# A hybrid HGRN2 / RWKV-7 / cross-attention layer on one core: six weight tiles taken in two passes over the tokens, one inverse product by halves, HGRN products regrouped, and a new order of all instructions

## The chip, the core and the metric

The kernel runs on one core of a Trainium2 chip. The metric is the device time of one execution in microseconds, the median over several runs. The engines are named as the profile names them: PE (TensorE, matrix products), PEld (its weight loads), DVE (VectorE), ACT (ScalarE), POOL (GpSimd) and SP (SyncE, which issues the DMAs).

## The reference, cut to what matters

One layer of a streaming encoder runs over a prompt of 1024 tokens and a sample of 32 tokens (1056 columns in all), width 1024, in fp32.

```python
def layer(x, mk, mv, hg_s0, rw_s0, shift0, lb, lw):
    n = rmsnorm(x, lw['norm_mix'])
    p = n @ lw['w_in']                                   # 1024 x 3840: HGRN columns, then RWKV columns
    hg_o, hg_s = hgrn2_mixer(p[..., :HG_COLS], ...)      # chunked recurrence, 4 heads of 128
    rw_o, rw_s, rw_shift = rwkv7_mixer(p[..., HG_COLS:], ...)   # 8 heads of 64; token shift, delta rule
    x = x + jnp.concatenate([hg_o, rw_o], axis=-1) @ lw['w_out']
    x = x + cross_attend(rmsnorm(x, lw['norm_cross']), mk, mv, lw['w_cq'], lw['w_co'])
    n = rmsnorm(x, lw['norm_ffn'])
    x = x + (jax.nn.silu(n @ lw['w_ff1']) * (n @ lw['w_ff3'])) @ lw['w_ff2']
    return x, hg_s, rw_s, rw_shift
```

`mk, mv` of the prompt are `rmsnorm(mem) @ w_k` and `@ w_v`. Both mixers carry a state from token to token; the RWKV one needs, per chunk of 64 tokens, the inverse of a triangular 64x64 matrix.

## The kernel before, in words

**Recording and planning.** The program is written as ordinary code on a `Graph`, which only records nodes. A PE node is a run of matmuls up to the next instruction of another engine or an explicit `cut`. `plan` then makes one list for every engine by simulating the five engines with fixed prices (`price`, `DELAY`): at each step it takes the ready node with the longest remaining path (`n.path`), with a bias per group of work (`BIAS`). `latest` turns a finished plan into latest start times, which serve as ranks of the next plan (`PASSES` times), and `nudged` adds a pseudo-random shift to the ranks of all nodes that are due after a given moment, one shift for each entry of `NUDGE` (moment, seed, reach). So these numbers set the order on every engine. On the chip every engine works its list strictly in that order. Because everything is emitted in one helper, all instructions carry one line number in the profile; groups are told apart by tiles and shapes. `f`, `mb`, `r`, `rw`, `wr` are regions of SBUF, `bank` is a bank of PSUM.

**Large products.** A weight tile of 128 columns (`load_w`) is fetched into `wr` (512 KB), rounded by ACT to fp32r (`hi`, in `rw`), and POOL computes the rest (`lo`, in `rw`). `gemm` adds three fp32r products for each k: hi·hi, hi·lo, lo·hi, so a tile of `w_in` takes 24 matmuls for each of the three token blocks of 352 (`BLOCKS`). There are two buffers each for `wr`, `hi` and `lo` (`FIFO`). `w_in` has 30 such tiles, 14 of which are RWKV ones; `rw_proj` mixes each block with the previous token (`mix`), which needs the last column of the block before (`edge`).

**Start.** `load_rows` fetches nine row tiles of x (128 tokens each, the last 32), takes the sum of squares on ACT, the power -1/2 on POOL (`rstd_pow`), scales by it and by the gain row `norm_mix` (a broadcast DMA of its own) on DVE, transposes on PE, and splits into hi (ACT) and lo (DVE).

**Mixers.** `lora` projects two RWKV tiles. `rwkv(j)` (j = 0, 2; two heads pairs each) first projects six tiles (r, k, v), then goes through five segments (four of 256 tokens, one of the sample's 32), each with a triangular `inverse` (five levels of small products, fp16 but for the last, which are fp32) and a serial chain over four chunks. `hgrn(i)` (i = 0..3) projects four tiles and goes through five segments as well; in a segment of 256 tokens it makes, for each of two groups of 128, one product of full size, two with 32 columns and one with 64.

**After the mixers.** `memory_kv` (fp32r, 256 columns; weights in `rw`), `out_proj` and `cross` (352 columns), the feed-forward part (264 columns), and the final norm. `memory_kv` may start once the regions that hold the normalized x are free, that is after the last projection of `w_in`; `out_proj` needs all mixers.

Of the kernel before, what the change touches and what calls it, by code (L numbers as in the profile page):

```python
# [21 lines left out]
KD = D // 128  # L22
# [12 lines left out]
LATER = 10.0  # L35
PASSES = 1
START, NUDGE = (291, 0.5), ((0, 3825, 0.6), (480, 1426, 0.2), (660, 4358, 1.5), (720, 1344, 0.6), (840, 6345, 3), (1200, 2280, 1.5), (1560, 9149, 3), (1620, 5315, 0.2), (1680, 6266, 12), (1740, 8928, 1.5),)
KEEP = 1.5 * BIAS
# [153 lines left out]
class Node:  # L192
    def __init__(self, graph, eng):
        self.eng, self.i = eng, len(graph.nodes)
        self.calls, self.cost, self.late = [], 0.0, 0.0
        self.preds, self.bufs, self.unit, self.bias, self.phase = {}, {}, graph.unit, graph.bias, graph.phase
        self.port = self.dense = False
        graph.nodes.append(self)
# [10 lines left out]
def shake(i, seed):  # L209

    return (i * 2654435761 + seed * 40503 * 65537 >> 7) % 1021 / 1020 if seed else 0.0
# [91 lines left out]
class Graph:  # L303
# [148 lines left out]
    def plan(self, rank):  # L452
# [29 lines left out]
        for n in nodes:  # L482
            n.path = n.path - n.bias + START[1] * shake(n.i, START[0]) if rank is None else -rank[n]
        engines = ("tensor", "vector", "scalar", "gpsimd", "sync")
# [223 lines left out]
class Net:  # L708
# [183 lines left out]
    def load_rows(self):  # L892
# [4 lines left out]
        gain = self.w2("grow")  # L897
        nc.sync.dma_start(gain, self.i["norm_mix"].to_broadcast([128, D]))
        for ap, n, t0 in self.rows():
# [579 lines left out]
    def mixers(self):  # L1479
        nc = self.nc  # L1480
        self.load_rows()
        self.params()
        self.last = self.mc.tile([128, 28], F32, name="last")
        self.lora()
        self.scratch_h()
        self.diag_n, self.diag = 0, []
# [44 lines left out]

    def proj(self, col, mix=None, bias=BIAS):

        nc = self.nc
        nc.bias = bias
        w = self.load_w(self.i["w_in"][0, :, col:col + 128], KD, eng=nc.gpsimd)

        def evac(t0, n, ps):
            t = self.tmp([128, TB], "pe")[:, :n]
            nc.scalar.copy(t, ps)  # L1540
            nc.sync.dma_start(self.p_dram[:, col // 128, t0:t0 + n], t)

        self.gemm(w, self.xact, KD, mix or evac)
        nc.bias = 0.0

    def rw_proj(self, tile, done=None, bias=BIAS):

        nc = self.nc
        V, S = nc.vector, nc.scalar
        mu, edge = self.P("mu", tile), None  # L1550

        def mix(t0, n, ps):
            nonlocal edge
            m = self.tmp([128, TB], "mixed")[:, :n]
            keep = self.P("omu", tile)
            c = min(TP - t0, n)
            if t0:
                S.activation(m[:, 0:1], ps[:, 0:1], AF.Identity, scale=keep, bias=edge)
                S.activation(m[:, 1:n], ps[:, 1:n], AF.Copy, scale=keep)
            else:  # L1560
                S.activation(m, ps, AF.Copy, scale=keep)
            V.scalar_tensor_tensor(m[:, 1:c], ps[:, 0:c - 1], mu, m[:, 1:c], ALU.mult, ALU.add)
            if c == n:
                edge = self.tmp([128, 1], "edge")
                S.activation(edge, ps[:, n - 1:n], AF.Copy, scale=mu)
# [9 lines left out]

        self.proj(2048 + 128 * tile, mix, bias)

# [29 lines left out]
    def rwkv(self, j):  # L1607
        nc = self.nc
        V, S, G, PE = nc.vector, nc.scalar, nc.gpsimd, nc.tensor
        half = (slice(0, 64), slice(64, 128))  # L1610
        for tile in (j, 4 + j, 8 + j):
            for a in range(2):
                self.rw_proj(tile + a)
        ht = None
# [206 lines left out]
    def inverse(self, am, nc_):  # L1821
# [26 lines left out]
        def product_diag(left, right):  # L1848
# [6 lines left out]
            return ps  # L1855

        def place(dst, ps, mask):
            V.tensor_tensor(dst.rearrange("p c (h u) -> p c h u", h=2),
                            ps.unsqueeze(2).to_broadcast([128, nc_, 2, 64]),
                            mask.unsqueeze(1).to_broadcast([128, nc_, 2, 64]), ALU.mult)  # L1860
# [12 lines left out]
        for l in range(1, 6):  # L1873
# [6 lines left out]
            if l < 5:  # L1880
                S.copy(x, ps)
        V.tensor_tensor(p, product(abd, y32), bc(self.i64), ALU.add)
        V.tensor_tensor(y1, product(xbd, p), y32, ALU.add)
# [9 lines left out]
    def hgrn(self, i):  # L1893
# [6 lines left out]
        for s in range(5):  # L1900
# [75 lines left out]
            for g in range(ng):  # L1976
# [4 lines left out]
                vk.append(self.u("hvk").rearrange("p (a u) -> p a u", a=2))  # L1981
                S.copy(vk[g][:m], ps[:m])
            for g in range(ng):
                gl = slice(128 * g, 128 * g + m)
                am = self.ah[self.ah_n % 3]
                self.ah_n += 1
                ams.append(am)
                ps = self.psm.tile([128, 128], F32, tag="m", name="ps_ha")
                PE.matmul(ps[:m, :m], lhsT=kg[:, gl], rhs=qg[:, gl], start=True, stop=True)
                if m == 128:  # L1990
                    PE.matmul(ps[0:32, 32:64], lhsT=kk[:, g, 0], rhs=qe[:, g, 1], start=True, stop=True)
                    PE.matmul(ps[64:96, 96:128], lhsT=kk[:, g, 2], rhs=qe[:, g, 3], start=True, stop=True)
                    PE.matmul(ps[0:64, 64:128], lhsT=kf[:, g].rearrange("p b u -> p (b u)"),
                              rhs=qf[:, g].rearrange("p b u -> p (b u)"), start=True, stop=True)
                V.copy_predicated(am[:m, :m], self.mask_h[:m, :m], ps[:m, :m])
            pkv = self.psm.tile([128, 2, 128], F32, tag="m", name="ps_kv")
# [63 lines left out]
```

## Time and profile before

| | |
|---|---|
| median of 3 runs | 1832.72 us (1831.22 to 1836.06) |
| the profiled execution | 1827.96 us, span 1826.2 us, mean granted clock 0.991 |
| PE busy | 1779.5 us, 97% of the span |
| PEld, DVE, ACT, POOL busy | 1681.4, 1264.6, 836.3, 605.7 us |
| PE waits, as the view of waits lists them | 18.3 us for DVE on `mb`, 12.3 of it at the very start |
| chain that ended last | 83% PE, 5% DVE, 3% ACT |

How to read it: busy time of PE includes time in which a pipelined matmul is stretched by a slower clock, so the granted clock has to be read beside it. The profiled execution is 4.8 us shorter than the median of the timed runs.

### The profile page before, as it was taken

What the parts mean: (1) busy time and instruction counts of PE and PEld (TensorE: products, weight loads), DVE (VectorE), ACT (ScalarE), POOL (GpSimd) and SP (SyncE); (2) the same over time, 40 slices, a digit from 0 to 9 for tenths busy, and PEclk for the clock granted to TensorE, in tenths of its full rate; (3) what the DMA queues carried; (4) which work ended last, traced back from release to release, by engine and by line L of the source; (5) the groups of instructions that cost most, each with busy time, mean ns of one, the idle gap of its engine ahead of it and who ended that gap; (6) DMA issues with size and microseconds to landing.
All of it is one profiled execution on the core that took longest, in us unless ns stands there. A gap on an engine that the chain in (4) does not pass through costs nothing.

```text
span 1826.2 us, 39245 instructions
## 1 busy us (share of the span) xinstructions
PE 1779.5 (97%) x15439; PEld 1681.4 (92%) x15439; DVE 1264.6 (69%) x2502; ACT 836.3 (46%) x1983; POOL 605.7 (33%) x764
## 2 busy tenths in 40 slices
PE   6999999999999989999999999999999999999997
PEld 5998888888989877999999999999999999999997
DVE  6246567867667879423554546998877877968996
ACT  5644446556454658533222346433333333653432
POOL 6234243443424434055000036632232223232321
PEclk9999999999999979999999999999999999999999
DMA  5244133332321346744111242232322234654522
GB/s 177 73 131 130 46 101 94 89 91 83 105 71 50 100 109 200 243 146 138 47 47 47 63 144 89 70 130 89 111 89 89 98 120 154 189 161 138 181 94 96
DMA packets 206313, 201.88 MB, mean 111 GB/s; under 512 B 18712, under 2 KB 191376, under 8 KB 206128
## 3 DMA queue, kind: packets, MB, share of 16 engines
q1 hardware_dynamic: 206128, 199.37, 35.0%
q8 instruction: 121, 1.98, 0.4%
q14 instruction: 64, 0.52, 0.1%
HBM read 139.66 MB, written 59.67 MB: 109 GB/s over the span
## 4 chain that ended last, share of the span: by engine, by line
PE 83%; DVE 5%; ACT 3%; DMA 2%; issue 1%; POOL 1%; SPq 0%; DVEq 0%; POOLq 0%; ACTq 0%
PE bank L383 83%; DVE f L383 2%; DVE mb L383 2%; ACT mb L383 2%; ACT f L383 1%; DVE rw L383 1%; DVE r L383 1%; DMA f<-p_scratch 1%; POOL mb L383 0%; ACT r L383 0%; POOL f L383 0%; ACT rw L383 0%; DMA f<-h_scratch 0%; DMA x_scratch<-mb 0%; DMA f<-in_cache_mem_k_dram 0%
## 5 line engine op out<-in xcount | busy, mean ns | idle before, releaser
L383 PE MATMUL bank<-r,rw 128*128 128x264 f32 (+1 forms) x5928 | 894.7, 305 | 4.3 <-POOL rw L383 2.0
L383 PEld LDWEIGHTS bank<-r,rw 128*128 128x128 f32 x5928 | 837.1, 188 | 13.3 <-POOL rw L383 3.2
L383 PE MATMUL bank<-mb,rw 128*128 128x264 f32 (+4 forms) x3672 | 509.6, 293 | 4.8 <-DVE r L383 1.9
L383 PEld LDWEIGHTS bank<-mb,rw 128*128 128x128 f32 x3672 | 484.2, 188 | 10.2 <-DVE rw L383 1.7
L383 DVE TENSOR_TENSOR f<-bank,f 128x264 f32<-128x264 f32 (+6 forms) x499 | 229.6, 472 | 192.6 <-PE bank L383 173.9
L383 POOL TENSOR_TENSOR f<-f 128x64 f32<-128x64 f32 (+8 forms) x205 | 115.4, 572 | 330.5 <-PE bank L383 187.8
L383 ACT CAST rw<-wr 128x512 fp32r<-128x512 f32 (+3 forms) x167 | 115.5, 697 | 211.0 <-PE bank L383 188.3
L383 DVE TENSOR_TENSOR f<-f 128x264 f32<-128x264 f32 (+8 forms) x309 | 188.5, 626 | 20.2 <-ACT f L383 13.1
L383 PE MATMUL bank<-f 128*128 128x128 f32 (+12 forms) x1374 | 193.6, 286 | 4.3 <-DVE f L383 2.5
L383 ACT ACTIVATE f<-f 128x256 f32<-128x256 f32 (+7 forms) x295 | 124.5, 447 | 114.0 <-DVE f L383 61.6
L383 PEld LDWEIGHTS bank<-f 128*128 128x128 f32 (+7 forms) x1262 | 141.5, 162 | 30.6 <-issue 6.6
L383 DVE TENSOR_TENSOR mb<-bank,f 128x1024 f16<-128x1024 f32 (+6 forms) x200 | 135.8, 705 | 44.5 <-PE bank L383 35.6
L383 PE MATMUL bank<-f,mb 64*64 64x64 f32 (+5 forms) x2248 | 122.9, 221 | 21.9 <-DVE mb L383 17.9
L383 ACT CAST rw<-r 128x512 fp32r<-128x512 f32 (+2 forms) x106 | 61.2, 577 | 116.7 <-PE bank L383 91.8
L383 DVE TENSOR_TENSOR rw<-wr,rw 128x512 fp32r<-128x512 f32 (+3 forms) x137 | 103.1, 757 | 16.5 <-ACT rw L383 15.6
L383 ACT COPY mb<-bank 128x512 f32<-128x512 f32 (+5 forms) x151 | 69.0, 467 | 89.8 <-PE bank L383 76.0
L383 POOL TENSOR_TENSOR rw<-wr,rw 128x1024 fp32r<-128x1024 f32 x30 | 72.5, 2418 | 96.6 <-ACT rw L383 66.1
L383 ACT COPY f<-bank 128x264 f32<-128x264 f32 (+8 forms) x221 | 76.0, 359 | 60.3 <-PE bank L383 44.9
L383 DVE TENSOR_TENSOR rw<-r,rw 128x512 fp32r<-128x512 f32 (+2 forms) x106 | 80.0, 755 | 23.0 <-ACT rw L383 22.2
L383 PEld LDWEIGHTS bank<-f,mb 64*64 64x64 f32 (+3 forms) x1352 | 62.1, 141 | 32.4 <-DVE mb L383 16.5
L383 ACT ACTIVATE mb<-bank,f 128x1 f32<-128x1 f32 (+5 forms) x133 | 55.4, 461 | 48.5 <-PE bank L383 45.5
L383 PE MATMUL bank<-mb 64*64 64x64 f32 (+5 forms) x1310 | 76.0, 237 | 1.1 <-ACT mb L383 1.0
(123 smaller groups left out, 1792.9 us busy)
## 6 DMA issues: line engine op xcount, KB each, us to landing
wr<-in_w_in_dram SPq DMA_DIRECT2D x30, 512.0 KB
wr<-in_w_ff_dram SPq DMA_DIRECT2D x28, 512.0 KB
p_scratch<-mb SPq DMA_DIRECT2D x80, 176.0 KB
f<-h_scratch SPq DMA_DIRECT2D x47, 264.0 KB
r<-in_w_ff_dram SPq DMA_DIRECT2D x24, 512.0 KB
h_scratch<-f SPq DMA_DIRECT2D x18, 528.0 KB
f<-x_scratch SPq DMA_DIRECT2D x15, 528.0 KB
f<-p_scratch SPq DMA_DIRECT2D x58, 128.0 KB
```

The lines of the kernel that those rows point to most:

```text
L383: getattr(eng, method)(*args, **kw)
```

## The change

`first` projects the six RWKV tiles of j = 0 in two passes: token block 0 of all six, then blocks 1 and 2 of all six. Each of these weight tiles is therefore fetched and split twice. `rwkv(0)` no longer projects. The last column of a block is kept per tile in `self.edges`. In `inverse`, the fp32 product with the block-diagonal matrix `abd` is made by two 64x64 products for each chunk instead of one 128x128 (68 chunks in all: eight full segments of 8, two of 2). In `hgrn`, the products of both groups go to one PSUM tile, all full-size ones first, then all with 32 columns, then all with 64. The DMA of the gain row gets a bonus in the plan (`soon`). `PASSES` goes from 1 to 4, and `NUDGE` from 10 entries to 41, with another start seed.

```diff
+SOON = 30
-PASSES = 1
-START, NUDGE = (291, 0.5), ((0, 3825, 0.6), (480, 1426, 0.2), (660, 4358, 1.5), (720, 1344, 0.6), (840, 6345, 3), (1200, 2280, 1.5), (1560, 9149, 3), (1620, 5315, 0.2), (1680, 6266, 12), (1740, 8928, 1.5),)
+PASSES = 4
...
-            n.path = n.path - n.bias + START[1] * shake(n.i, START[0]) if rank is None else -rank[n]
+            n.path = n.soon + (n.path - n.bias + START[1] * shake(n.i, START[0]) if rank is None else -rank[n])
...
-        nc.sync.dma_start(gain, self.i["norm_mix"].to_broadcast([128, D]))
+        nc.sync.dma_start(gain, self.i["norm_mix"].to_broadcast([128, D])).soon = SOON
...
         self.last = self.mc.tile([128, 28], F32, name="last")
+        self.edges = {}
         self.lora()
+        self.first(BLOCKS[:1], BLOCKS[1:])
...
-                S.activation(m[:, 0:1], ps[:, 0:1], AF.Identity, scale=keep, bias=edge)
+                S.activation(m[:, 0:1], ps[:, 0:1], AF.Identity, scale=keep, bias=self.edges[tile])
...
-        self.proj(2048 + 128 * tile, mix, bias)
+        self.proj(2048 + 128 * tile, mix, bias, blocks)
+
+    def first(self, *groups):
+
+        for blocks in groups:
+            for tile in (0, 1, 4, 5, 8, 9):
+                self.rw_proj(tile, bias=0.0, blocks=blocks)
...
-        for tile in (j, 4 + j, 8 + j):
-            for a in range(2):
-                self.rw_proj(tile + a)
+        if j:
+            for tile in (j, 4 + j, 8 + j):
+                for a in range(2):
+                    self.rw_proj(tile + a)
...
+        def halves_product(left, right):
+
+            ps = stacked()
+            for c in range(nc_):
+                for hf in half:
+                    PE.matmul(ps[hf, c], lhsT=left[hf, c, hf], rhs=right[hf, c], start=True, stop=True)
+            nc.cut()
+            return ps
...
-        V.tensor_tensor(p, product(abd, y32), bc(self.i64), ALU.add)
+        V.tensor_tensor(p, halves_product(abd, y32), bc(self.i64), ALU.add)
...
+            psh = self.psm.tile([128, 2, 128], F32, tag="m", name="ps_ha")
             for g in range(ng):
                 gl = slice(128 * g, 128 * g + m)
+                PE.matmul(psh[:m, g, :m], lhsT=kg[:, gl], rhs=qg[:, gl], start=True, stop=True)
+            if m == 128:
+                for g in range(ng):
+                    PE.matmul(psh[0:32, g, 32:64], lhsT=kk[:, g, 0], rhs=qe[:, g, 1], start=True, stop=True)
+                    PE.matmul(psh[64:96, g, 96:128], lhsT=kk[:, g, 2], rhs=qe[:, g, 3], start=True, stop=True)
+                for g in range(ng):
+                    PE.matmul(psh[0:64, g, 64:128], lhsT=kf[:, g].rearrange("p b u -> p (b u)"),
+                              rhs=qf[:, g].rearrange("p b u -> p (b u)"), start=True, stop=True)
+            for g in range(ng):
                 am = self.ah[self.ah_n % 3]
...
-                V.copy_predicated(am[:m, :m], self.mask_h[:m, :m], ps[:m, :m])
+                V.copy_predicated(am[:m, :m], self.mask_h[:m, :m], psh[:m, g, :m])
```

The new seeds change the order nearly everywhere. Three places follow.

On SP, at the very start of the program (x rows, the gain row, weight tiles). Before:

```order
L383 DMA mb_87<-in_x_prompt_dram 128x1024 x3
L383 DMA mb_87<-in_norm_mix_dram 128x1024
L383 DMA mb_87<-in_x_prompt_dram 128x1024
L383 DMA wr_75<-in_w_in_dram 128x8x128 x2
L383 DMA mb_87<-in_x_prompt_dram 128x1024 x3
```

Now:

```order
L384 DMA mb_87<-in_norm_mix_dram 128x1024
L384 DMA mb_87<-in_x_prompt_dram 128x1024 x4
L384 DMA wr_75<-in_w_in_dram 128x8x128
L384 DMA mb_87<-in_x_prompt_dram 128x1024
L384 DMA wr_75<-in_w_in_dram 128x8x128
L384 DMA mb_87<-in_x_prompt_dram 128x1024 x3
```

The gain row moved from the fourth place to the first, and each x row is one place later behind it.

On PE, one HGRN segment of 256 tokens late in the mixers (rows with 32x32 and the 64x64 row right behind them are its 32- and 64-column products; the `bank<-mb 64x64 x4` row ahead belongs to the RWKV chain). Before:

```order
L383 MATMUL bank_58<-mb_87 64x64 x4
L383 MATMUL bank_61<-f_0_71 128x128
L383 MATMUL bank_61<-mb_87,f_0_71 32x32 x2
L383 MATMUL bank_61<-mb_87 64x64
L383 MATMUL bank_62<-f_0_71 128x128
L383 MATMUL bank_62<-mb_87,f_0_71 32x32 x2
L383 MATMUL bank_62<-mb_87 64x64
L383 MATMUL bank_64<-mb_87,f_0_71 128x512
```

Now:

```order
L384 MATMUL bank_61<-f_0_71 128x128 x2
L384 MATMUL bank_60<-f_0_71 128x128 x2
L384 MATMUL bank_60<-f_0_71 32x32 x4
L384 MATMUL bank_60<-f_0_71 64x64 x2
L384 MATMUL bank_65<-f_0_71,mb_87 64x64 x4
```

Two rounds through the three sizes became one round in one bank.

On PE, the end of the projections of `w_in` (rows with 128x352 are projections, `128x64` with `f,mb` are products of `inverse`). Before:

```order
L383 MATMUL bank_60<-r_0_79,rw_83 128x352 x2
L383 MATMUL bank_60<-r_0_91,rw_83 128x352
L383 MATMUL bank_60<-r_0_79,rw_83 128x352
L383 MATMUL bank_62<-f_0_71,mb_87 128x128
L383 MATMUL bank_58<-f_0_71,mb_87 128x128
L383 MATMUL bank_62<-f_0_71,mb_87 128x128
L383 MATMUL bank_58<-f_0_71,mb_87 128x128
```

Now:

```order
L384 MATMUL bank_64<-mb_87,f_0_71 128x512
L384 MATMUL bank_59<-r_0_79,rw_83 128x352
L384 MATMUL bank_59<-r_0_91,rw_83 128x352
L384 MATMUL bank_59<-r_0_79,rw_83 128x352 x2
L384 MATMUL bank_59<-r_0_91,rw_83 128x352
L384 MATMUL bank_59<-r_0_79,rw_83 128x352 x2
L384 MATMUL bank_59<-r_0_91,rw_83 128x352
L384 MATMUL bank_59<-r_0_79,rw_83 128x352 x2
L384 MATMUL bank_59<-r_0_91,rw_83 128x352
L384 MATMUL bank_59<-r_0_79,rw_83 128x352
L384 MATMUL bank_63<-f_0_71 128x128 x2
L384 LDWEIGHTS mb_87
```

Before, the first products of the last full RWKV segment (its rows `f,mb 128x128`) come only after the last projection; now the last projection already stands between products of that segment's `inverse` (the row after these is `bank_62<-f_0_71,mb_87 128x64`). From the last row with 128x352 to the first row of `memory_kv` (`rw,r 128x256`), the order of PE before has 601 small matmuls, and now 254.

More of the change, by code (lines that the diff above doesn't have):

```diff
@@ L35 @@
 LATER = 10.0
-PASSES = 1
-START, NUDGE = (291, 0.5), ((0, 3825, 0.6), (480, 1426, 0.2), (660, 4358, 1.5), (720, 1344, 0.6), (840, 6345, 3), (1200, 2280, 1.5), (1560, 9149, 3), (1620, 5315, 0.2), (1680, 6266, 12), (1740, 8928, 1.5),)
+SOON = 30
+PASSES = 4
+START, NUDGE = (4291, 2), ((0, 3475, 0.2), (35, 7729, 1.5), (65, 3475, 0.2), (205, 9903, 3), (210, 1329, 0.2), (235, 4113, 0.6), (265, 1329, 0.2), (530, 1329, 0.2), (560, 9269, 0.6), (660, 4719, 0.6), (665, 8473, 0.2), (670, 9328, 12), (685, 7830, 12), (700, 636, 0.2), (705, 6641, 12), (710, 2682, 12), (715, 1121, 0.6), (720, 8195, 12), (800, 1255, 12), (845, 148, 0.6), (860, 7859, 6), (870, 6519, 0.2), (890, 8853, 12), (915, 8563, 12), (950, 7902, 12), (975, 5479, 6), (1025, 3786, 6), (1045, 3924, 6), (1090, 3786, 6), (1165, 6074, 0.2), (1235, 3786, 6), (1480, 3201, 1.5), (1540, 9428, 3), (1555, 3786, 6), (1580, 3609, 1.5), (1590, 9225, 6), (1610, 5077, 3), (1665, 1872, 1.5), (1680, 878, 6), (1740, 2277, 6), (1770, 1679, 1.5),)
 KEEP = 1.5 * BIAS
@@ L195, in __init__ @@
         self.calls, self.cost, self.late = [], 0.0, 0.0
-        self.preds, self.bufs, self.unit, self.bias, self.phase = {}, {}, graph.unit, graph.bias, graph.phase
+        self.preds, self.bufs, self.unit, self.bias, self.phase, self.soon = {}, {}, graph.unit, graph.bias, graph.phase, 0.0
         self.port = self.dense = False
@@ L1530, in s, with proj @@
         return self.sp.tile([128, 128 if dt == F32 else 256], dt, tag="s", name=name)
-    def proj(self, col, mix=None, bias=BIAS):
+    def proj(self, col, mix=None, bias=BIAS, blocks=BLOCKS):
         nc = self.nc
@@ L1541, in evac, with rw_proj @@
             nc.sync.dma_start(self.p_dram[:, col // 128, t0:t0 + n], t)
-        self.gemm(w, self.xact, KD, mix or evac)
+        self.gemm(w, self.xact, KD, mix or evac, blocks)
         nc.bias = 0.0
-    def rw_proj(self, tile, done=None, bias=BIAS):
+    def rw_proj(self, tile, done=None, bias=BIAS, blocks=BLOCKS):
         nc = self.nc
         V, S = nc.vector, nc.scalar
-        mu, edge = self.P("mu", tile), None
+        mu = self.P("mu", tile)
         def mix(t0, n, ps):
-            nonlocal edge
             m = self.tmp([128, TB], "mixed")[:, :n]
@@ L1563, in mix @@
             if c == n:
-                edge = self.tmp([128, 1], "edge")
+                edge = self.edges[tile] = self.tmp([128, 1], "edge")
                 S.activation(edge, ps[:, n - 1:n], AF.Copy, scale=mu)
@@ L1987, in hgrn @@
                 ams.append(am)
[L1988 to L1994, printed above, removed]
-                V.copy_predicated(am[:m, :m], self.mask_h[:m, :m], ps[:m, :m])
+                V.copy_predicated(am[:m, :m], self.mask_h[:m, :m], psh[:m, g, :m])
             pkv = self.psm.tile([128, 2, 128], F32, tag="m", name="ps_kv")
```

## The prediction

> **What bounds the kernel.** I read the page first, then the waits of PE, then PE by windows.
>
> ```profile
> span 1826.2 us, 39245 instructions
> PE 1779.5 (97%) x15439; PEld 1681.4 (92%) x15439; DVE 1264.6 (69%) x2502; ACT 836.3 (46%) x1983; POOL 605.7 (33%) x764
> PE bank L383 <- DVE mb L383: 18.3, 10, 12.3
> PE bank L383 <- DVE f L383: 4.9, 10, 1.1
> PE bank L383 <- DVE r L383: 3.5, 5, 1.3
> PE bank L383 <- ACT mb L383: 3.3, 6, 1.0
> PE bank L383 <- ACT f L383: 2.7, 6, 0.9
> PE bank L383 <- POOL rw L383: 2.0, 2, 1.2
> ```
>
> PE is busy for 97% of the span, and the six rows of waits (us in total, times, longest) add up to 34.7 us. So a microsecond of work taken from PE is a microsecond of time, and work put on ACT, POOL or the DMAs costs something only where PE then waits. A busy PE is not always a fast one, though, so the windows come next (length; PE, PEld, DVE, ACT and POOL busy; granted clock; DMA share and GB/s):
>
> ```profile
> 600.00:623.00 23.00, 22.89 (x200) 18.56 (x198) 18.60 (x40) 18.72 (x47) 13.19 (x18) 1.00 0.29 83
> 645.00:652.00 7.00, 5.32 (x69) 4.29 (x68) 6.93 (x11) 5.86 (x21) 2.47 (x4) 0.98 0.75 206
> 652.00:679.00 27.00, 23.59 (x176) 18.72 (x173) 18.32 (x60) 12.32 (x47) 9.06 (x32) 0.50 0.38 103
> 623.07:706.37 83.30, 75.42 (x923) 60.36 (x922) 71.57 (x198) 55.08 (x179) 32.13 (x81) 0.84 0.41 116
> 1040.00:1400.00 360.00, 358.09 (x2926) 356.75 (x2925) 280.27 (x452) 147.94 (x308) 135.58 (x103) 1.00 0.31 103
> ```
>
> Almost everywhere PE is full at clock 1.00 (the first and the last row). The exception is 623.07 to 706.37, the end of the mixers: the projections have run out, `memory_kv` has not begun, and PE lives on the small products of the last segments, which wait for DVE and ACT. It loses twice there: 83.30 - 75.42 = 7.9 us of idle time, and 27 us at half clock, whose 23.59 busy us would be 11.8 at full clock. The stretch thus holds 75.42 - 11.8 = 63.6 us of work and lasts 83.3: 19.7 us are lost. This is the largest loss of the kernel behind its start.
>
> **The change part by part.**
>
> *Inverse product by halves.* These rows stand side by side (start, duration, columns of the array, shape, count; a fp32 product leaves two records, and the next row's start tells when it is over):
>
> ```profile
> 591.37 1.15 PE L383 MATMUL bank<-f,mb 64*64 64x64 f32 x32
> 592.44 0.71 PE L383 MATMUL bank<-f 128*128 128x128 f32 x4
> ...
> 595.24 1.89 PE L383 MATMUL bank<-mb 128*128 128x64 f32 x16
> 596.97 0.40 PE L383 MATMUL bank<-f 128*128 128x64 f16 x8
> ```
>
> The product with `abd` is the third row: eight matmuls, 596.97 - 595.24 = 1.73 us. Sixteen 64x64 ones, the first row, take 592.44 - 591.37 = 1.07 us. That saves 0.66 us in each of eight full segments and, with a quarter of the matmuls, about 0.16 in each of two small ones: -5.6 us, all on PE. The bounds: -8 if the halves overlap better than in that row, -3 if entering and leaving the 64x64 shape costs more between full-size products. [...]
>
> *HGRN products regrouped.*
>
> ```profile
> 597.67 0.49 PE L383 MATMUL bank<-f 128*128 128x128 f32 x2
> 598.09 0.26 PE L383 MATMUL bank<-mb,f 128*32 128x32 f32 x4
> 598.27 0.33 PE L383 MATMUL bank<-mb 128*64 128x64 f32 x2
> 598.53 0.49 PE L383 MATMUL bank<-f 128*128 128x128 f32 x2
> 598.95 0.26 PE L383 MATMUL bank<-mb,f 128*32 128x32 f32 x4
> 599.13 0.33 PE L383 MATMUL bank<-mb 128*64 128x64 f32 x2
> 599.39 1.12 PE L383 MATMUL bank<-mb,f 128*128 128x512 f32 x2
> ```
>
> One round of three sizes takes 598.53 - 597.67 = 0.86 us, two take 1.72. Within a run of one size a narrow product costs 1.07 / 16 = 0.07 us by the row of 32 above, so the second group's three narrow ones add 0.21 to the first round. The full one takes 598.09 - 597.67 = 0.42 with the change of size behind it; as an estimate I put half of that on the product, 0.21. So 1.72 becomes 0.86 + 0.42 = 1.28, -0.44 us in each of 16 segments: -7.0 us. If changes of size were free, it would be 0; if the second group were free, -13.8. I stay in the middle, since 0.86 is about twice what its products come to. The first group's result now waits 0.4 us longer for its `copy_predicated` on DVE, with the DVE work queued behind it; PE has the projections to do meanwhile.
>
> *Six tiles in two passes.* PE makes the same matmuls. New are six DMAs of 512 KB on SP, six hi casts on ACT and six lo subtractions on POOL:
>
> ```profile
> L383 POOL TENSOR_TENSOR rw<-wr,rw 128x1024 fp32r<-128x1024 f32 x30 | 72.5, 2418 | 96.6 <-ACT rw L383 66.1 <-PE bank L383 30.2
> 14.77 1.05 ACT L383 CAST rw<-wr 128x1024 fp32r<-128x1024 f32 x1
> L383 PE MATMUL bank<-r,rw 128*128 128x352 f32 x2736 | 478.1, 328 | 3.3 <-POOL rw L383 2.0 <-DVE r L383 0.9
> 36.00:100.00 64.00, 63.18 (x395) 61.61 (x396) 21.85 (x55) 36.15 (x93) 13.53 (x11) 1.00 0.27 82
> ```
>
> POOL's 6 x 2.42 = 14.5 us and ACT's 6.3 us fall into the window 36 to 100, where POOL is busy for 13.5 of 64 us, and 3 MB are little at 82 GB/s. What is tight is the turnover. A tile in the first pass feeds PE for only 24 x 478.1 / 2736 = 4.2 us, and with two buffers the next hi and lo can start only when an older tile is done: 1.05 + 2.42 = 3.5 us, plus handing over. That just fits. Bounds: 0, and 6 x 1.2 = 7.2 us if each tile waits as long as PE's longest wait for `rw` (1.2, shown above). I take +1, near to the fit.
>
> What it buys: the first segment of `rwkv(0)` needs block 0 only, so the recurrences start about 50 us of projections earlier (six tiles times two blocks of 4.2 us), and stand beside projections to their end. In the new order 254 small matmuls instead of 601 lie between the last projection and `memory_kv`. In proportion that is 63.6 x 254 / 601 = 27 us of work. The other 37 us move forward and lie among groups of 352 columns, as in the window 600 to 623, where PE is full. If the loss shrinks with the work, 19.7 x 254 / 601 = 8 us stay and 12 are gained. The bounds: 19.7 gained, if neither wait nor half clock remains, and 0, if one half-clock period of 27 us (worth 13.6) and 6 us of waits come back on the shorter stretch. I take -12. Next late there are the last inverse's own steps on DVE and ACT, which have no projection beside them for 6 us of PE work.
>
> *Gain row sooner.*
>
> ```profile
> 4.24 2.32 POOL L383 TENSOR_SCALAR_AFFINE_SELECT f<-f 64x64 f32<-64x64 f32 x5
> 4.57 1.06 ACT L383 ACTIVATE mb<-mb 128x1024 f32<-128x1024 f32 x1 [2.51 <-DMA mb<-in_x_prompt_dram]
> 7.38 0.19 POOL L383 TENSOR_SCALAR f<-f 128x1 f32<-128x1 f32 x1
> 7.81 0.55 POOL L383 TENSOR_TENSOR f<-f 128x1 f32<-128x1 f32 x1
> 10.95 1.28 DVE L383 SCALAR_TENSOR_TENSOR mb<-mb,f 128x1024 f32<-128x1024 f32 x1 [4.13 <-DMA mb<-in_norm_mix_dram]
> 12.29 5.08 PE L383 MATMUL bank<-f,mb 128*128 128x128 f32 x24 [12.29 <-DVE mb L383]
> 18.71 3.22 POOL L383 TENSOR_TENSOR rw<-wr,rw 128x1024 fp32r<-128x1024 f32 x1
> 26.12 1.86 PE L383 MATMUL bank<-r,rw 128*128 128x352 f32 x10 [1.20 <-POOL rw L383]
> ```
>
> DVE waits for the gain row until 10.95, though POOL had the row's factor at 8.36. With the gain row first that wait goes, and POOL is late next: in its new list 14 selects of 64x64 stand ahead of the first factor, not 10, so at 0.46 us each (the first row) it comes 1.9 us later, the scaling at some 10.3 and PE at some 11.6: -0.7 us. Behind that the first matmuls still wait for POOL's lo, whose place in POOL's list hardly changes. I take -1, with -3 and +2 as ends.
>
> *The new order elsewhere.* No work goes or comes. Of the 34.7 us of waits some 17 are at the start and 7.5 in the stretch above, so 10 are left to gain, and as much could be lost: 0, with 8 either way.
>
> **The sum:** -5.6 - 7.0 + 1 - 12 - 1 + 0 = -24.6 us on a span of 1826.2, so 1801.6, or 1803.4 for the profiled execution, which took 1827.96. The median of the runs was 1832.72, 4.8 us above it; it becomes 1832.7 - 24.6 = 1808.1, so 1808.
>
> **The rivals.** *The end of the mixers gains nothing* (20%): the half clock sets in again and the waits are as long, because fewer products wait for the same chain. For it: in the row 645 to 652 a PE only 5.32 / 7.00 busy was enough to bring on half clock. Against it: less than half of that work is left. Then 1808 + 12 = 1820.
>
> *The clock stays full* (15%): the short stretch never gets thin enough, and little waits. Then the remaining 8 us go too: 1800. [...]
>
> *Slower* (6%): the first pass starves PE. If hi and lo of a tile take 5.4 us rather than 3.5 (POOL's 3.22 us of 18.71 above, behind its other work), PE waits 1.2 us in every 5.4; that is as thin as the row 645 to 652, and projections would run at half clock for 27 us, which costs 13.6. With the 7.2 us of waits this is +20.8 instead of +1. It decides only where the end of the mixers gains nothing either: -5.6 - 7.0 + 20.8 - 1 = +7.2, 1840. Above 13.6 us it outweighs what the other steps take from PE.
>
> *No change* (4%): the same with two thirds of it.
>
> **How the numbers follow.** 55% for 1808 with a range of its own of 1798 to 1819, and the others as given. The measurement tells 0.3%, 5.5 us, from no change. The first three cases are faster by more: 90%; 4% within, 6% slower. The range for 8 in 10 leaves out the slower cases and the best tenth: 1789 to 1824.
>
> **What would show it.** Right: PE busy falls by some 20 us; rows of 64*64 64x64 with 32 records stand where 128*128 128x64 f32 x16 stood; in HGRN, rows 128*128 x4, 128*32 x8, 128*64 x4 follow each other in about 1.28 us; from the last 352-column projection to the first 256-column matmul less than 40 us pass; the first PE row starts before 12.3. Wrong: waits of PE for POOL `rw` or ACT `rw` between 45 and 90 above 7 us in total; a second window of clock 0.50; or waits spread over the mixers, which would mean that the new order is tight where the prices are wrong.

## The result, and the profile after

The changed kernel takes 1803.29 us (median of four runs, 1803.02 to 1803.93) beside 1834.39 us for the kernel before (four runs, 1831.22 to 1836.55). The ratio is 0.983, 95% interval 0.982 to 0.985: 31 us faster. The forecast was 1808, in a range of 1789 to 1824. The profiled execution has a span of 1801.6 us; 1826.2 was 24.6 us longer, which is the forecast sum to the tenth. That the sum came out does not make its terms right, as the experiments show.

The head of the page of after, and the view of PE's waits (total us, times, longest us):

```profile
span 1801.6 us, 39539 instructions
PE 1760.8 (98%) x15575; PEld 1669.0 (93%) x15575; DVE 1275.2 (71%) x2502; ACT 842.1 (47%) x1989; POOL 621.8 (35%) x770
PE bank L384 <- DVE mb L384: 17.4, 9, 11.6
PE bank L384 <- DVE f L384: 4.8, 8, 1.4
PE bank L384 <- POOL rw L384: 3.4, 2, 1.8
PE bank L384 <- ACT mb L384: 2.5, 4, 1.2
PE bank L384 <- ACT f L384: 1.5, 4, 0.6
PE bank L384 <- DMA mb<-in_x_sample_dram: 1.3, 1, 1.3
PE bank L384 <- DVE rw L384: 0.8, 1, 0.8
```

PE's busy time fell by 18.7 us. The waits fell by less: all rows of the view add up to 32.4 us, against 37.4 of before (31.7 in the seven rows shown here, 34.7 in the six that the prediction shows). So the larger part of the gain is work (or slow work) that is gone from PE, not waiting.

The windows of after, with the columns as before; the third row is the stretch from the last projection to the first `memory_kv` matmul, the fourth its part at half clock:

```profile
36.00:100.00 64.00, 62.03 (x415) 59.17 (x413) 27.72 (x56) 43.22 (x97) 29.75 (x26) 1.00 0.57 171
600.00:641.47 41.47, 39.83 (x528) 35.08 (x528) 37.40 (x75) 26.64 (x68) 18.80 (x27) 1.00 0.27 74
641.47:676.70 35.23, 30.84 (x414) 23.74 (x412) 30.58 (x102) 25.58 (x91) 14.39 (x39) 0.90 0.41 120
652.90:659.70 6.80, 6.20 (x52) 4.24 (x52) 5.32 (x23) 4.40 (x18) 3.81 (x15) 0.50 0.30 92
```

The stretch lasts 35.2 us instead of 83.3, and half clock in it 6.8 us instead of 27.3. By the prediction's own reckoning 30.84 - 6.20 / 2 = 27.7 us of it are work and 7.5 are lost, where 19.7 were.

Rows of after in order of time (start, duration, columns of the array, shape, records). The first two pieces are an HGRN segment and a halves product; the row behind each tells when it is over. The last two pieces are the first pass and the start:

```profile
325.00 0.60 PE L384 MATMUL bank<-mb,f 128*128 128x128 f32 x4
325.54 0.32 PE L384 MATMUL bank<-f,mb 128*32 128x32 f32 x8
325.78 0.45 PE L384 MATMUL bank<-mb 128*64 128x64 f32 x4
326.16 0.49 PE L384 MATMUL bank<-f 128*128 128x128 f32 x2
...
587.84 1.15 PE L384 MATMUL bank<-mb 64*64 64x64 f32 x32
588.92 4.09 PE L384 MATMUL bank<-r,rw 128*128 128x352 f32 x24
...
65.80 3.80 PE L384 MATMUL bank<-r,rw 128*128 128x352 f32 x22 [1.63 <-POOL rw L384]
69.43 0.60 PE L384 MATMUL bank<-f,mb 128*128 128x128 f32 x4
69.78 4.09 PE L384 MATMUL bank<-r,rw 128*128 128x352 f32 x24
...
11.64 1.97 PE L384 MATMUL bank<-f,mb 128*128 128x128 f32 x8 [11.64 <-DVE mb L384]
14.74 1.97 PE L384 MATMUL bank<-f,mb 128*128 128x128 f32 x8 [1.13 <-DVE mb L384]
18.45 3.40 PE L384 MATMUL bank<-f,mb 128*128 128x128 f32 x16 [1.74 <-DVE mb L384]
21.60 0.57 PE L384 MATMUL bank<-r,rw 128*128 128x352 f32 x2
23.98 6.29 PE L384 MATMUL bank<-r,rw 128*128 128x352 f32 x28 [1.81 <-POOL rw L384]
```

The HGRN products now take 326.16 - 325.00 = 1.16 us, the halves 588.92 - 587.84 = 1.08. In the first pass PE waits once for POOL, 1.63 us, and from there a tile follows on a tile. At the start PE begins 0.65 us sooner, waits 4.7 us for the next rows and the first weights, and is at the projections no sooner than before, where this row starts them:

```profile
20.93 3.99 PE L383 MATMUL bank<-r,rw 128*128 128x352 f32 x14
```

### A ledger of PE's list

To see where a kernel loses, every matmul record of a trace was put beside its place in PE's list, and each pair of neighbouring matmuls was priced with the median time from start to start that the same pair has in the trace of before. The sum of the prices is the work of a list; what it took longer is lost, to waits, half clock or slower neighbours. The columns follow the program, since the same moment is another place in another order: to 40 us, from there to the last projection, the stretch up to the first `memory_kv` matmul, from there to the first `out_proj` matmul, and the rest (us, one profiled execution each):

| kernel | median | work | to 40 us | mixers | stretch | memory | rest | lost in all |
|---|---|---|---|---|---|---|---|---|
| before | 1834.4 | 1728.1 | 9.9 | 27.9 | 21.8 | 1.3 | 16.5 | 77.5 |
| after | 1803.3 | 1710.4 | 10.4 | 34.1 | 10.2 | 5.3 | 12.1 | 72.1 |
| whole | 1809.5 | 1716.0 | 9.2 | 35.0 | 10.1 | 5.4 | 12.0 | 71.8 |
| rounds | 1808.0 | 1716.7 | 10.7 | 32.9 | 10.3 | 4.6 | 11.9 | 70.4 |
| both | 1814.1 | 1722.3 | 9.2 | 33.9 | 10.2 | 3.3 | 11.7 | 68.2 |
| oldseeds | 1862.6 | 1709.8 | 12.5 | 50.6 | 11.7 | 7.4 | 49.5 | 131.8 |
| nofirst | 1848.0 | 1709.3 | 9.2 | 40.4 | 26.0 | 7.7 | 31.4 | 114.7 |
| nofirst_oldseeds | 1842.3 | 1712.7 | 12.4 | 35.0 | 20.4 | 3.3 | 35.2 | 106.3 |
| b_newseeds | 1886.7 | 1722.9 | 9.1 | 54.5 | 21.9 | 8.8 | 42.8 | 137.2 |
| with_first | 1827.0 | 1712.9 | 10.5 | 40.7 | 16.0 | 5.0 | 19.0 | 91.4 |
| without_first | 1841.3 | 1711.9 | 9.3 | 41.7 | 30.4 | 3.6 | 24.2 | 109.1 |
| bwarm | 1833.6 | 1730.5 | 9.5 | 28.6 | 16.4 | 1.3 | 18.7 | 74.5 |
| after_t | 1805.1 | 1709.2 | 9.2 | 36.6 | 10.2 | 5.6 | 12.9 | 74.7 |

The work of `whole`, `rounds` and `both` stands 5.6, 6.3 and 11.9 us above that of after, close to what their times show below.

Neither the work nor the losses hold the time ahead of PE's first matmul (12.3 us in before, 11.6 in after) and from the start of its last one on (8.4 and 7.4). The columns are also less exact than their digits. A pair that before has only in its half-clock period is priced at half clock, and most of the other kernels have some 60 pairs that do not occur in before at all. Priced instead by the same pairs outside half clock, in the traces of all these kernels, before has 1719.1 us of work and loses 10.0, 32.9, 24.5, 2.6 and 16.4 us in the order of the columns, after 1707.4 and 10.4, 36.5, 10.0, 6.2 and 11.9, and `both` has 1717.1 of work. So a difference of less than some 4 us between two rows of the table should not be relied on.

### The profile page after: what moved, and what is told of

Read it like the earlier page. It is cut to its first block, busy times and chain, and to the rows that moved or that the text cites. A ratio compares the mean times of both kernels' runs of the same rounds, so it can differ in the third digit from the quotient of the medians.

```text
span 1801.6 us, 39539 instructions
## 1 busy us (share of the span) xinstructions
PE 1760.8 (98%) x15575; PEld 1669.0 (93%) x15575; DVE 1275.2 (71%) x2502; ACT 842.1 (47%) x1989; POOL 621.8 (35%) x770
## 5 line engine op out<-in xcount | busy, mean ns | idle before, releaser
L384 PE MATMUL bank<-mb,rw 128*128 128x264 f32 (+3 forms) x3648 | 503.1, 293 | 1.0 <-DVE f L384 0.7
L384 DVE TENSOR_TENSOR f<-bank,f 128x264 f32<-128x264 f32 (+8 forms) x563 | 264.2, 485 | 188.4 <-PE bank L384 167.3
L384 DVE TENSOR_TENSOR f<-f 128x264 f32<-128x264 f32 (+8 forms) x351 | 228.4, 667 | 16.5 <-ACT f L384 9.0
L384 POOL TENSOR_TENSOR f<-f 128x264 f32<-128x264 f32 (+8 forms) x211 | 118.3, 572 | 313.0 <-DMA x_scratch<-f 194.6
L384 ACT CAST rw<-wr 128x1024 fp32r<-128x1024 f32 (+3 forms) x168 | 120.0, 718 | 209.7 <-PE bank L384 167.5
L384 PEld LDWEIGHTS bank<-f 128*128 128x128 f32 (+6 forms) x1276 | 138.3, 162 | 29.7 <-issue 7.2
L384 DVE TENSOR_TENSOR mb<-bank,f 128x256 f32<-128x256 f32 (+6 forms) x180 | 119.0, 688 | 37.1 <-PE bank L384 24.3
L384 ACT COPY mb<-bank 128x512 f32<-128x512 f32 (+6 forms) x161 | 72.2, 461 | 82.8 <-PE bank L384 73.3
L384 POOL TENSOR_TENSOR r<-r 128x512 f32<-128x512 f32 (+2 forms) x46 | 64.9, 1418 | 119.5 <-DMA r<-in_w_ff_dram 62.2
L384 ACT COPY f<-bank 128x264 f32<-128x264 f32 (+9 forms) x219 | 74.9, 362 | 59.4 <-PE bank L384 52.2
L384 PEld LDWEIGHTS bank<-f,mb 64*64 64x64 f32 (+5 forms) x1258 | 59.4, 138 | 30.9 <-DVE mb L384 17.7
L384 PE MATMUL bank<-mb,f 64*64 64x64 f32 (+10 forms) x622 | 80.7, 299 | 2.1 <-DVE f L384 1.0
```

What stands on the lines that cost most here:

```text
L384: getattr(eng, method)(*args, **kw)
```

## The experiments

**The work on PE, in the order of after.** `after_again` is the changed kernel, run on the chip of the next three. `whole` and `rounds` leave every list as the planner made it and swap only what is issued for a node: the halves become the whole product again, the HGRN products go back to two rounds. `both` does both.

```diff
 # emit (all three)
-                for method, args, kw in node.calls:
+                for method, args, kw in getattr(node, "instead", None) or node.calls:
 # whole: halves_product
                     PE.matmul(ps[hf, c], lhsT=left[hf, c, hf], rhs=right[hf, c], start=True, stop=True)
+            nc.open.instead = [("matmul", (ps[:, c],), dict(lhsT=left[:, c], rhs=right[:, c], start=True, stop=True)) for c in range(nc_)]
             nc.cut()
 # rounds: hgrn, behind the eight products
+                made = nc.open.calls
+                nc.open.instead = made[:-8] + [made[k - 8] for k in (0, 2, 3, 6, 1, 4, 5, 7)]
```

> The changed kernel itself, run beside the three below so that each can be set against it on one chip: 1803 us, as before, to within 1 us. No theory expects anything else.

> The changed kernel with its order of all instructions kept, but the last fp32 product of the inverse made again by one 128x128 product for each chunk instead of two of 64x64. Theory (the gain is PE work taken away, and PE has no slack there): the product of a full segment goes from 1.08 us to about 1.73 us, 8 x 0.65 + 2 small = +5.6 us, so 1809 us (1806 to 1811); PE's busy time rises by the same 5 to 6 us and the waits stay. Rival (the gain is a better order, the halves only fill what would be waiting): within 1.5 us of the changed kernel, 1802 to 1804.5, the longer product eating into the wait behind it.

> The changed kernel with its order kept, but the HGRN products of a full segment made again in two rounds (full size, 32, 32, 64 columns of one group, then of the other) instead of all of one size together. The same products in all. Theory (each change of the array's size costs PE time): from about 1.28 us to 1.72 us for each of 16 segments, +7.0 us, 1810 us (1807 to 1814). Rival (the grouping costs nothing by itself, what changed the time is the order around it): within 1.5 us of the changed kernel.

> Both of the edits above together, again in the order of the changed kernel. Theory (both are PE work on a path without slack, so they add): +12.6 us, 1816 us (1812 to 1820), and what is then left of the gain against the kernel before, some 15 us, is the end of the mixers and the order. Rival (they hide in each other's waits): less than 8 us above the changed kernel. Rival (order only): within 2 us of the changed kernel.

Measured: `after_again` 1802.78 us (1801.97 to 1803.62; ratio to before 0.983, 0.981 to 0.985), `whole` 1809.52 (1807.59 to 1812.56; 0.987, 0.985 to 0.989), `rounds` 1807.96 (1807.91 to 1810.53; 0.986, 0.985 to 0.988), `both` 1814.05 (1811.39 to 1821.18; 0.990, 0.988 to 0.992). So the halves are worth 6.7 us, the regrouping 5.2, both 11.3, nearly their sum. The medians mix granted clocks a little; among the runs at clock 0.997 alone (two each, one of `both`) it is 5.9, 5.8 and 9.9 us. The waits do not take it up: the losses of the four stand within 4 us of each other. The rows that answer, first of `whole`:

```profile
591.79 1.98 PE L384 MATMUL bank<-mb 128*128 128x64 f32 x16
593.58 0.73 PE L384 MATMUL bank<-r,rw 128*128 128x352 f32 x3
```

and of `rounds`, the segment shown above of after:

```profile
325.79 0.38 PE L384 MATMUL bank<-mb,f 128*128 128x128 f32 x2
326.10 0.26 PE L384 MATMUL bank<-f,mb 128*32 128x32 f32 x4
326.28 0.33 PE L384 MATMUL bank<-mb 128*64 128x64 f32 x2
326.54 0.49 PE L384 MATMUL bank<-mb,f 128*128 128x128 f32 x2
326.96 0.26 PE L384 MATMUL bank<-f,mb 128*32 128x32 f32 x4
327.14 0.33 PE L384 MATMUL bank<-mb 128*64 128x64 f32 x2
327.40 0.49 PE L384 MATMUL bank<-f 128*128 128x128 f32 x2
```

The whole product takes 593.58 - 591.79 = 1.79 us where the halves take 1.08; over the eight segments 1.70 to 1.83 against 1.08 in each. The same eight HGRN products take 327.40 - 325.79 = 1.61 us in two rounds and 1.16 in one; the medians over the 16 segments are 1.65 and 1.23. Both theories stand: this is PE work with nothing to hide it.

**Code and seeds crossed.** Four kernels, to tell what `first` does from what the new shifts do.

```diff
 # oldseeds: after with the numbers of before
-PASSES = 4
-START, NUDGE = (4291, 2), (41 entries)
+PASSES = 1
+START, NUDGE = (291, 0.5), (10 entries)
 # nofirst: after without the two passes, with its own numbers
-        self.first(BLOCKS[:1], BLOCKS[1:])
-        if j:
-            for tile in (j, 4 + j, 8 + j): ...
+        for tile in (j, 4 + j, 8 + j): ...
 # nofirst_oldseeds: both of these; b_newseeds: before with PASSES, START and NUDGE of after
```

> All code of the change, but with the one pass of planning, the start seed and the ten shifts of the kernel before. Between the last projection and the first memory matmul PE's list then has 242 small matmuls (601 in the kernel before, 254 in the changed one). Theory (the end of the mixers gains by `first`, which lets that small work go earlier beside projections): the stretch stays as short as in the changed kernel, 34 to 40 us, and the time is 1803 plus what waits the unsuited shifts leave elsewhere, 0 to 8 us: 1808 us (1803 to 1813). Rival (the new shifts made the gain of the stretch): the stretch loses 20 us again and the time is 1814 to 1820.

> The changed kernel without `first` (the six tiles are projected in one pass over the tokens at the head of rwkv(0), as before), with its own passes and shifts. 482 small matmuls are left between the last projection and the first memory matmul. Theory (what a stretch loses goes with the small matmuls left in it: 21.8 us for 601, 10.2 us for 254): about 18 us lost there, +7.6 us, less about 1 us for the second fetch and split saved: 1810 us (1806 to 1815). Rival (`first` is worth nothing there): 1802 to 1804.

> The changed kernel without `first` and with the passes and shifts of the kernel before; so only the halves, the HGRN regrouping and the gain row's bonus are left. 421 small matmuls between the last projection and the first memory matmul. Theory (losses by the small matmuls left there): about 16 us lost in the stretch, +5.5 us against the changed kernel, and 0 to 8 us of waits elsewhere: 1811 us (1806 to 1818). Against the kernel before that is -12.6 us of PE work and about -6 us in the stretch. Rival (the stretch and the waits go by seeds alone): 1821, the kernel before less the PE work.

> The kernel before with the four passes, start seed and 41 shifts of the changed one, and nothing else of it. 283 small matmuls between the last projection and the first memory matmul. Theory (losses by the small matmuls left there): the stretch loses some 11 us instead of 21.8, so -10 us, and 0 to +8 us of waits elsewhere: 1826 us (1822 to 1833). Rival (shifts fit only the code they were chosen for): 1834 to 1845, waits for DVE or POOL spread over the mixers.

Measured: `oldseeds` 1862.62 us (1861.88 to 1864.03; ratio 1.017, 1.015 to 1.019), `nofirst` 1848.03 (1845.47 to 1854.47; 1.009, 1.008 to 1.011), `nofirst_oldseeds` 1842.26 (1838.24 to 1844.76; 1.005, 1.004 to 1.007), `b_newseeds` 1886.68 (1885.36 to 1888.73; 1.030, 1.028 to 1.032). All four expectations missed by 30 to 60 us, and on the same side: any code with shifts that were not chosen for it is slower than either kernel, although the three that keep the new products have 15 to 19 us less work than before by the ledger. Where it goes is seen best where nothing was changed, from `out_proj` on. The waits of PE behind 1000 us in `oldseeds`:

```profile
PE bank L384 <- DVE rw L384: 8.6, 6, 3.6
PE bank L384 <- ACT rw L384: 7.0, 4, 2.9
PE bank L384 <- DVE f L384: 4.2, 5, 1.6
PE bank L384 <- ACT f L384: 2.1, 1, 2.1
```

and behind 980 us in after:

```profile
PE bank L384 <- DVE f L384: 0.7, 2, 0.5
PE bank L384 <- DVE r L384: 0.2, 1, 0.2
```

The same feed-forward code waits 22 us in one order and 1 in the other, 16 of it for what DVE and ACT write into `rw`, its weights, and five short periods at half clock, 20.5 us in all, go with it from `out_proj` on (granted clock 0.98 from 1400 us on, 0.99 in after). So the passes, the start seed and the shifts together are worth some 60 us to the code they were chosen for (1862.6 against 1803.3), twice the gain of the whole change, and these four kernels say little on a part of the code by its time. By place they say something: with `first`, after and `oldseeds` lose 10.2 and 11.7 us in the stretch; without it, before and the three others lose 20.4 to 26.0, whatever the shifts. And the loss does not go with the number of small matmuls left there: 283 in `b_newseeds` cost 21.9 us, 601 in before 21.8.

**Half clock and short waits.** `bwarm` is the kernel before with 15 matmuls more, laid into the waits ahead of the half clock.

```diff
+FILL = {5068: 1, 5106: 1, 5126: 2, 5134: 7, 5152: 4}    # number in PE's list: how many ahead of it
...
+                    if node.eng == "tensor":
+                        for _ in range(FILL.get(done, 0)):
+                            real.tensor.matmul(args[0], lhsT=ident, rhs=ident[:, :64], start=True, stop=True)
+                        done += 1
                     getattr(eng, method)(*args, **kw)
```

> The kernel before, in its own order, with 15 more fp32 matmuls of 128x128 by 64 columns on PE (0.22 us each, 3.4 us in all), put ahead of five matmuls for which PE waited between 646 and 658 us (1, 1, 2, 7 and 4 of them ahead of waits of 0.37, 0.33, 0.48, 1.60 and 1.02 us). Their results are overwritten by the matmul behind them; no other engine waits for them. Theory (the half clock from 651.7 to 679.0 us sets in because PE is thinly busy just before): the clock stays at 1.00 or falls for one or two records of 3.4 us as in the changed kernel (6.8 us), and the stretch is 7 to 12 us shorter: 1820 to 1827 us against 1832 to 1834. Rival (the clock is halved by something that short waits have no part in): 27 us at half clock as before and the time within 2 us of the kernel before, or up to 3 us above it for the added work.

Measured: 1833.64 us (12 runs, 1826.59 to 1839.41) beside 1831.97 (17 runs, 1827.77 to 1837.28), ratio 1.001, 0.9996 to 1.002. The windows of `bwarm`:

```profile
651.70:662.00 10.30, 9.08 (x107) 8.02 (x107) 10.19 (x24) 7.85 (x26) 2.17 (x8) 1.00 0.57 139
662.00:675.70 13.70, 13.38 (x94) 9.96 (x96) 8.05 (x33) 5.14 (x25) 5.90 (x22) 0.50 0.38 105
```

In the profiled execution, one of the two fastest of the twelve, the half clock comes 10.3 us later and lasts 13.7 us instead of 27.3; the stretch is 3 us shorter. But over the runs the mean granted clock is 0.9893 against 0.9885 of the kernel before, and no time is gained. So in this execution filling the waits moved the half clock and did not do away with it. It fits neither theory cleanly: in order of time PE had just run 10.3 us with 9.08 busy and no wait above 0.37 us (the row below) when it set in at 662.0:

```profile
660.98 0.39 PE L389 MATMUL bank<-f,mb 128*128 128x64 f16 x8 [0.37 <-DVE f L389]
```

The runs of these two kernels yield a price, though. Over the 17 of before, the time falls by 1.07 us for each 0.001 of mean granted clock (correlation -0.88); over the 12 of `bwarm` by the same 1.07 (-0.91). As 0.50 is the only other value of the granted clock in the traces of before and after, 0.001 of 1832 us is 3.7 us at half clock: as an estimate, from run to run one us more at half clock goes with 0.29 us more time.

**`first`, in orders sought for each code.** To compare with and without `first` fairly, both got four passes and shifts sought anew, from none, for 40 minutes each: random shifts were kept where the planner's own end came sooner. `after_t` adds 15 shifts found in this way to the 41 of after.

```diff
 # with_first: all code of after
-START, NUDGE = (4291, 2), (41 entries)
+START, NUDGE = (4291, 2), ((10, 6282, 1.5), (120, 2630, 0.6), (160, 2122, 0.6), (330, 4265, 3), (400, 6991, 6), (1480, 2690, 6))
 # without_first: the code of nofirst
+START, NUDGE = (4291, 2), ((0, 6220, 0.6), (720, 7371, 3), (830, 5171, 6), (855, 2373, 3), (920, 24, 12), (975, 6837, 12), (995, 3289, 3), (1440, 2492, 3))
```

> All code of the change, but instead of its 41 shifts six others, found by 40 minutes of trying shifts at random and keeping those by which the plan's own last instruction came sooner, from none at all. 288 small matmuls between the last projection and the first memory matmul. It is to be set against without_first, whose shifts were sought in the same way for as long. Theory (`first` is worth the shorter stretch, some 10 us, wherever the order suits the code): 1810 to 1816 us, 10 to 16 us below without_first. Rival (what the stretch gains is lost again among the mixers): within 4 us of without_first.

> The changed code without `first`, with eight shifts sought in the same way and for as long as those of with_first. 376 small matmuls between the last projection and the first memory matmul. Theory (`first` is worth the shorter stretch): 1822 to 1830 us; 15 to 22 us are lost in the stretch, against 9 to 12 in with_first. Rival (the stretch's gain is lost again among the mixers, and its place does not matter): 1808 to 1818, like with_first.

> The changed kernel with its 41 shifts kept and 15 more among them, sought in the same way. Theory (the order still holds some 60 us of losses, and a plan that ends sooner also runs sooner): 1797 to 1801 us against 1803, a little better than both kernels. Rival (the plan's prices are no finer than this, and what it gains is not seen on the chip): 1802 to 1806.

Measured: `with_first` 1826.97 us (1824.72 to 1831.01; ratio 0.997, 0.995 to 0.998), `without_first` 1841.32 (1838.33 to 1843.27; 1.004, 1.003 to 1.005), `after_t` 1805.10 (1804.52 to 1809.07; 0.985, 0.984 to 0.986). Both of the first two came out 11 us above their ranges, so such a short search does not reach the 41 shifts; but they stand 14.4 us apart, and the ledger shows where: 30.4 against 16.0 us lost in the stretch, the mixers ahead of it within 1 us (the rest differs by 5, though `first` changes nothing there; in the profiled executions the two are 17.7 apart, since that of `without_first` is the slowest of its five, at clock 0.981 against 0.984 to 0.986). The stretch in the windows, first of `with_first`:

```profile
645.40:688.40 43.00, 34.18 (x444) 26.81 (x444) 35.98 (x102) 29.90 (x99) 14.77 (x42) 0.80 0.26 78
```

and of `without_first`, with the part at half clock:

```profile
645.10:705.80 60.70, 50.20 (x546) 39.43 (x545) 46.58 (x130) 37.01 (x120) 18.32 (x51) 0.63 0.22 63
653.70:698.10 44.40, 35.73 (x363) 28.22 (x361) 33.82 (x98) 26.52 (x87) 15.09 (x44) 0.50 0.17 48
```

The theory holds for this pair as far as the place goes: with little more work in it (30.3 us against 27.0 by the ledger), the stretch without `first` spends 44.4 us at half clock, the one with it 17.1. The time of one pair proves less, as each code had one search only. `after_t` does not beat after: a plan that ends 2 us sooner by the planner's prices is 2 us later on the chip. Nor is that the only such case: the plan of `without_first` ends at 1788.7 us and that of before at 1793.2, but on the chip `without_first` is 7 us behind before. The changed kernel remains the fastest of all.

## Why the prediction was right, and where only its sum was

*Halves, -5.6.* Right: 6.7 us, inside the bounds of 3 and 8, or 5.9 at equal clock. The product costs 1.08 us in every full segment, between full-size neighbours too, and the 128x64 product, taken as 1.73 throughout, came to 1.70 to 1.83. These rows go from start to start, so they hold the change of shape behind the product and not the one ahead of it. Counted from the start of the matmul ahead of it, a segment takes 1.20 to 1.33 us with the halves in after and 1.81 to 1.93 in `whole`, 0.53 to 0.65 less, where the rows alone say 0.62 to 0.75. The change ahead thus costs some 0.1 us, and the eight full segments gain 4.7 us on PE, where the prediction counted 8 x 0.66 = 5.3 for them.

*HGRN, -7.0.* Right in mechanism, 5.2 us measured as time, or 5.8 at equal clock. The products themselves went from 1.65 to 1.23 us in the median, 0.42 a segment where 0.44 was forecast; 16 x 0.42 = 6.7. The other 1.5 us are within what the runs of `rounds` differ by (2.6).

*Two passes, +1.* Right in kind. PE waited 1.6 us for POOL `rw` between 36 and 100 us, and the ledger finds 2.0 us more lost between 40 and 80. POOL had the cover that was named: it was busy 29.75 of the 64 us, 16.2 more than before.

*End of the mixers, -12.* The number was hit: 7.5 us stay lost by the prediction's reckoning, 8 were forecast. The reason was half right. That `first` brings it is borne out by place: 10.1 to 16.0 us are lost in every order with it, 20.4 to 30.4 in every one without, but for `bwarm`, where the added matmuls bring it down to 16.4. By time it rests on one pair (14.4 us, some 5 of which lie behind the mixers). That the loss shrinks in proportion to the small matmuls left is wrong: 283, 376, 421, 482 and 601 of them lost 21.9, 30.4, 20.4, 26.0 and 21.8 us without `first`. And the gain does not stay whole: in the ledger after loses 6.2 us more than before among the mixers and 4.0 more in `memory_kv`, where the work that was moved away now stands (3.6 and 3.6 by the prices outside half clock). Up to `out_proj` after loses 60.0 us against 60.9, or 63.1 against 70.0 by those prices, so most of what the stretch gained is gone again, or half of it. "The other 37 us move forward and lie among groups of 352 columns, as in the window 600 to 623, where PE is full" is therefore the step that failed: with the work there, 7 to 10 us more are lost. Whether moving the work costs this or the new order does is not shown; between `with_first` and `without_first`, the mixers lose 1.0 us less with `first` and `memory_kv` 1.4 more.

*Gain row, -1.* PE began at 11.64 us, forecast 11.6. But nothing is left of it at 40 us: with the time ahead of PE's first matmul, 11.6 + 10.4 = 22.0 us are lost by then, and 12.3 + 9.9 = 22.2 before. POOL was late next, as forecast. The first weights' lo came 2 us later: it let PE go on at 23.98 us, where before it was done at 18.71 + 3.22 = 21.93. Of the x rows only the first three went one place later on SP. No run leaves out the bonus of the gain row alone.

*Order elsewhere, 0.* Right only as a sum. Outside the other terms, the 10.2 us lost among the mixers and in `memory_kv` stand against 4.4 us less lost from `out_proj` on, 1 us less from PE's last matmul on, and less work than `both` takes back: 17.7 - 11.9 = 5.8 us by the table, 1719.1 - 1717.1 = 2.0 by the prices outside half clock. Where that work went stays open; it is not fewer changes of the array's size, since PE's list of `both` has 440 of them and that of before 431. Nothing in the prediction weighs these against each other, so that they come to about nothing, and the sum to the tenth, is luck. The bounds of 8 either way held for two orders that had both been chosen for their code. For one that had not, they were off by a factor of seven.

*The median.* 1808 was 4.7 too high, because the 4.8 us by which before's median exceeded its profiled execution were carried over. That excess goes with half clock: the runs of before differ in it (mean clock 0.985 to 0.991 in 17 runs), those of after hardly do (0.995 to 0.997 in eight). From 0.9885 to 0.996 is, by the slope over the runs, 7.5 x 1.07 = 8 us of the 31 gained; in the profiled executions (0.991 to 0.996) it is 5.

*The rivals.* "The clock stays full" and "nothing gained" both gave way to something between: 6.8 us at half clock. "Slower" named a starving first pass, which did not come. The way to a slower kernel that the runs do show, an order that does not suit the code, was not among them: it should have been, as it cost 60 us in `oldseeds`.

*The signs.* All that were named for a right prediction came. Of those for a wrong one, waits spread over the mixers came in part: from 40 us to the last projection, the view of waits has 8.4 us in after and 5.0 in before.

## What to carry to other kernels

Here, with PE busy for 97 to 98% of the span, the halves and the grouping of small products by array size were worth about what the rows said (6.7 and 5.2 us in the medians, 5.6 and 7.0 forecast), and nearly added up (11.3 for both). In a program whose order is searched, an edit and its order are one thing: an edit tried with the old order can look 30 us slower and be 31 us faster with its own, so compare code only in orders sought equally for both, and expect several us of chance even then. A ledger that prices work by a trace should leave out the stretches at a slower clock (before has 1728.1 us of work by the prices with them, 1719.1 without). When runs of one kernel differ, look at the granted clock of each: here it went with the spread, and a forecast made on one execution has to say how much half clock that one had.

## What the hardware showed that was not expected

- From run to run, each us at half clock went with 0.29 us more time (an estimate, from the slope over 17 runs of before and 12 of `bwarm`), not the half that the prediction took (13.6 us for 27; by this price 7.9). Inside the periods about half is lost all the same: by the prices outside half clock, 13.9 of 27.3 us in before, 6.7 of 13.7 in `bwarm`, 26.4 of 44.4 in `without_first`. One row shows it directly: the whole product of `abd` at 658.14 us in before took 661.75 - 658.14 = 3.61 us at clock 0.50, the one at 595.24 took 1.73 at clock 1.00. A part of these losses is waits for other engines (3.4 us in before, 0.3 in `bwarm`, 8.7 in `without_first`), and what of them would come at full clock too does not count between runs. That this is why the two prices differ is argued, not shown.
- Half clock set in with PE 88% busy: at 662.0 us in `bwarm`, behind 10.3 us with 9.08 busy and no wait above 0.37. In before no wait between 641 and 651.7 us, where it set in, was above 0.56; the longest of the stretch, 1.60 us, ended at 655.51, when the clock was at 0.50 already. The prediction laid half clock to a thin PE (5.32 of 7.00 us busy); what sets it in stays open. Small products among projections did not bring it on: from 600.00 to 641.47 us in after the clock was 1.00, with PE busy 39.83 of 41.47.
- The periods at half clock that end inside the span last 3.41 and 27.31 us in before, 3.41 and 6.83 in after; the one in the stretch lasts 13.7 in `bwarm` and 44.4 in `without_first`. Within rounding these are 1, 8, 1, 2, 4 and 13 times 3.41.
- Sixteen fp32 products of 64x64 in a row took 1.07 to 1.09 us from their start to that of the next product of another shape, at clock 1.00, in before, after and `rounds` alike: 0.07 us each, against 1.73 / 8 = 0.22 for one of 128x128 by 64 columns.
